# Local heads' scores as single fp32 matmuls on unsplit q and k, and two key tiles instead of four for the sample

## The chip, the cores and the metric

The kernel runs on one core of one Trainium2 chip. The metric is the time of one execution in device microseconds; lower is better. All arithmetic of the reference is in fp32.

## The reference

One encoder layer is applied to two requests, a prompt of 1024 tokens and a sample of 256, each with the same 16 learned meta tokens in front. The model width is 2048, a head has 128 channels. Eight heads (A) attend to all tokens of their request, with two key/value heads; eight heads (B, "local") attend to the meta tokens and to a window of 8 rows by 16 columns around the token, on a grid 64 columns wide. The sample has four rows, so its window is all rows by 16 columns.

```python
def encoder_layer(h, ...):                       # h: (B, N, 2048), N = 16 + tokens
    u = rms_norm(h, norm_w) @ w_in               # 2048 x 6656
    qa, ka, va, za, qb, kb, vb, zb = split(u)
    qa, ka = rope(rms_norm(qa)), rope(rms_norm(ka))          # per head
    ya = global_gqa(qa, ka, va) * silu(za)
    qb, kb = rms_norm(qb), rms_norm(kb)                      # per head
    yb = neighbourhood_attention(qb, kb, vb, rpb) * silu(zb)
    return h + concatenate([ya, yb]) @ w_out

def attend(qb, kidx, bidx):                      # in neighbourhood_attention
    s_win = einsum('bqhd,bqwhd->bhqw', qb, kx[:, kidx]) * scale + rpb_flat[:, bidx]
    s_meta = einsum('bqhd,bkhd->bhqk', qb, km) * scale
    p = softmax(concatenate([s_meta, s_win]))
    return p_meta @ vm + p_win @ vx[:, kidx]
```

## The kernel before

The host reorders tokens into strips of eight columns and puts them in two chunks: chunk 1 has the sample (256 tokens), the first 240 tokens of the prompt and the meta tokens, 512 in all; chunk 2 has the other 784 tokens of the prompt. For each chunk the projection runs over strips of 128 output channels (`strips`, L204 to L206), which are the columns of one head for q, k, v or z. The result of a strip is normalised on the way out of PSUM (`qk_evac`, `v_rows`, `z_evac`).

Most products on TensorE are made of three. An fp32 operand is split into a high half `hi` (a ScalarE copy to the type fp32r, L56) and a low half `lo` (VectorE's difference, L57); the product is `hi hi + hi lo + lo hi`. So there are three matmuls per product in the projection, in the scores and in the output projection (L920 to L922). Some products are done on unsplit fp32 operands in one matmul instruction: P·V of the local heads (L405 for the sample, L465 for the prompt), and the transposes of V (L246, L486).

Attention is interleaved with the projection. The sample's attention runs in chunk 1, head by head after its strips; that of the local heads is `attend_sample`. It cuts the 64 columns of the grid into four windows of 16 query columns (64 queries each) with 32 key columns (128 keys, starting at `32 * w0` for `w0` in `WIN0 = (0, 1, 3, 4)`), which overlap: four key tiles, each with three matmuls of 64 queries (L380 to L382), and V turned to key-major form by one transpose per window (L246). The scores on the meta tokens are three matmuls more (`meta_scores`, L266 to L268).

The prompt's local heads run in `attend_strip`, in 32 blocks: eight heads with four windows each. A block has four key tiles `t`; tiles 0 and 3 meet 128 queries, tiles 1 and 2 meet 192. Each takes three matmuls, L431 to L433, which read q as strided pieces of 64 columns. P·V is one fp32 matmul for each tile, L465. The local heads' q and k of chunk 2 are stored unsplit in DRAM (`q2d`, `k2d`), those of chunk 1 split (`qd`, `kd`); `k_load` and `q_load` fetch both parts for one head, and `split_in_place` (L752, L753) splits the 784 columns of chunk 2. Pools `k`, `q` and `tab` have one buffer each in this half. The last head's four blocks run between the first eight steps of the output projection.

The softmax's largest value and sum go through a reduction over partitions on GpSimd (L278, L295). A TileContext with a scheduler decides the order of the instructions on each engine and in the DMA queue, which all DMAs share (SP); PSUM has two buffers for scores (`sp`), one for P·V (`op`) and one for transposes (`tp`).

Of the kernel before, what the change touches and what calls it, by code (L numbers as in the profile page):

```python
# [38 lines left out]
QB = 256  # L39
WIN0 = (0, 1, 3, 4)  # L40
WTYPE = (0, 1, 1, 2)
FILL = 1
# [7 lines left out]
class Kern:  # L50
# [320 lines left out]

    def attend_sample(self, q, zs, k, meta, vals, vmeta, tab, ydst):

        nc = self.nc
        qh, ql = q[:, 0, :], q[:, 1, :]
        ps = self.sp.tile([P, 2, QB], F32, tag="sp", name="sp")
        for w, w0 in enumerate(WIN0):
            o, c = 32 * w0, slice(64 * w, 64 * w + 64)
            kh, kl = k[:, 0, o:o + P], k[:, 1, o:o + P]
            nc.tensor.matmul(ps[:, 0, c], kh, qh[:, c], start=True, stop=False)  # L380
# [4 lines left out]
        s = s[:, 0, :]  # L385
        for i in range(2):

            v = slice(128 * i, 128 * i + 128)
            nc.vector.scalar_tensor_tensor(out=s[:, v].rearrange("p (w c) -> p w c", w=2),
                                           in0=ps[:, 0, v].rearrange("p (w c) -> p w c", w=2),  # L390
                                           scalar=SCALE, in1=tab[:, i:i + 2, 64:128], op0=ALU.mult, op1=ALU.add)
        m1 = self.t.tile([P, QB], F32, tag="t", name="m1")
        nc.vector.tensor_copy(m1[:], s)
        ma = self.all_max(m1, sm)
        nc.vector.tensor_tensor(out=s, in0=s, in1=ma[:], op=ALU.subtract)
        nc.scalar.activation(s, s, AF.Exp)
        pm3 = self.meta_probs(sm, ma, 1.0)
        a1 = self.t.tile([P, QB], F32, tag="t", name="a1")
        nc.vector.tensor_copy(a1[:], s)
        tot = self.all_sum(a1, sm)  # L400
        po = self.op.tile([P, QB], F32, tag="po", name="po")
        nc.tensor.matmul(po[:], vmeta, pm3[:], start=True, stop=False)
        for w in range(4):
            c = slice(64 * w, 64 * w + 64)
            nc.tensor.matmul(po[:, c], vals[:, w, :], s[:, c], start=False, stop=w == 3)  # L405
        self.put_y(po, tot, zs, ydst)

    def attend_strip(self, q, zs, k, meta, vals, vmeta, tab, w, ydst):

        nc = self.nc
        qv = q[:].rearrange("p i (g r) -> p i g r", g=4)[:, :, :, 64 * w:64 * w + 64]
        groups = {0: (0, 2), 3: (2, 4), 1: (0, 3), 2: (1, 4)}
        pa = self.sp.tile([P, 2, QB], F32, tag="sp", name="sp")
# [9 lines left out]
        for t in (0, 3, 1, 2):  # L425
            a, e = groups[t]
            dst = part(pa, pb, t)
            o = NMETA + 256 * t + 32 * WIN0[w]
            kh, kl = (k[:, i, o:o + P] for i in range(2))
            qh, ql = (qv[:, i, a:e, :] for i in range(2))  # L430
            nc.tensor.matmul(dst, kh, qh, start=True, stop=False)  # L431
            nc.tensor.matmul(dst, kh, ql, start=False, stop=False)
            nc.tensor.matmul(dst, kl, qh, start=False, stop=True)  # L433
            if t == 3:
# [33 lines left out]

    def bias_table(self, h):

        tab = self.tab.tile([P, 3, 384], F32, tag="bt", name="bt")
        with self.tc.issue_after(self.lastw):
            self.nc.sync.dma_start(tab[:], self.io["bt"][h])
        return tab
# [85 lines left out]
    def chunk1(self):  # L560
# [10 lines left out]
        PM = NS + C1P  # L571

        def k_strip(s, g, wc, rope):
            kt_ = self.k.tile([P, 2, T1], F32R, tag="k1", name="kc1")
# [8 lines left out]
        def v_strip(s, g):  # L583
            loc = g > 1
            vs = self.v.tile([P, 4, P], F32 if loc else F32R, tag="v0", name="vs")
# [61 lines left out]
        for h in range(8):  # L647
            kj, qj = k_strip(KB + h, 2 + h, kwb, False), q_strip(QB_ + h, 8 + h, qwb, False)
            k, = pr(kj)
# [5 lines left out]
            else:  # L655
                (v, vm), z = pr(vj, zj)
            run(8 + h, q, z, k, v, vm, self.bias_table(h))


    def chunk2(self):  # L660
# [88 lines left out]

        def split_in_place(t):  # L750

            nc.scalar.copy(t[:, 0], t[:, 1].bitcast(F32))  # L752
            nc.vector.tensor_tensor(out=t[:, 1], in0=t[:, 1].bitcast(F32), in1=t[:, 0].bitcast(F32), op=ALU.subtract)  # L753

        def k_load(g):
            k, km = k_first(g)
            nc.sync.dma_start(k[:, 1, K0:].bitcast(F32), self.k2d[g][:])
            split_in_place(k[:, :, K0:])
            return k, km

        def q_load(h):
            q = self.q.tile([P, 2, NP], F32R, tag="q", name="q")
            nc.sync.dma_start(q[:, :, :C1P].bitcast(F32), self.qd[h][:])
            nc.sync.dma_start(q[:, 1, C1P:].bitcast(F32), self.q2d[h][:])
            split_in_place(q[:, :, C1P:])
            return q

# [8 lines left out]
        def run_block(h, b, q, z, k, v, tab):  # L776
            k, km = k
            v, vm = v
            if tab is not None:
                c = slice(64 * b, 64 * b + 64)  # L780
                self.attend_strip(q, strips_of(z[:])[:, :, c], k, km, v[b], vm[:], tab, b,
                                  strips_of(self.yd[h][:, :NP])[:, :, c])
# [9 lines left out]
        def local_blocks():  # L792
            for h in range(NH):
                k, v = k_load(2 + h), v_windows(h)
                tab, q, z = self.bias_table(h), q_load(8 + h), z_load(8 + h)
                for b in range(4):
# [226 lines left out]
    def build(self):  # L1023
# [3 lines left out]
        with tc.tile_pool(name="dr", bufs=1, space=DRAM) as dp, tc.tile_pool(name="const", bufs=1) as cp, \  # L1027
                tc.tile_pool(name="raw", bufs=3) as self.raw, tc.tile_pool(name="w", bufs=4) as self.w:
            self.kd = [dp.tile([P, 2, NMETA + C1P], F32, name=f"kd{g}") for g in range(10)]
            self.vn = [dp.tile([NP, P], F32, name=f"vn{g}") for g in range(10)]  # L1030
            self.vmd = [dp.tile([M3, P], F32, name=f"vmd{g}") for g in range(10)]
            self.qd = [dp.tile([P, 2, C1P], F32, name=f"qd{h}") for h in range(16)]
            self.zd = [dp.tile([P, NP], F32, name=f"zd{h}") for h in range(16)]
# [11 lines left out]
            with ExitStack() as ps, ExitStack() as es_y:  # L1045
# [22 lines left out]
                pool(es_proj, "ev", 8, side="right", **kw)  # L1068
                for name, bufs in (("k", 1), ("v", 1), ("tab", 1), ("q", 1), ("z", 1), *work, ("y", 1)):
                    pool(es_attn, name, bufs, **kw)  # L1070
# [54 lines left out]


def _lay(x):
    return np.ascontiguousarray(x.reshape(x.shape[0], KT, P).transpose(2, 1, 0))
# [33 lines left out]
```

## Time and profile before

| what | value |
|---|---|
| median of 3 runs | 2222.22 us (2219.42 to 2223.22) |
| profiled execution | 2220.95 us |
| its span | 2219.1 us |
| VectorE busy | 74% of the span |
| ScalarE busy | 51% |
| GpSimd busy | 24% |
| TensorE's granted clock, mean | 0.998 |
| bytes moved by DMA | 391.21 MB |

The span runs from the first to the last instruction; what lies around it is 1.85 us. In the profile PE is TensorE's matmul, PEld its loading of weights (which runs beside PE), DVE is VectorE, ACT ScalarE, POOL GpSimd and SP the engine that issues the DMAs. A group of instructions is named by its line, its engine, what it writes and reads (`out<-in`) and its shape. Durations of matmuls overlap, since the engine is pipelined. In the chain of work that ended last, each piece lasts from the end of the piece before it to its own.

### The profile page before, as it was taken

The numbers are of one execution on the slowest core, as the hardware profiler recorded it, in microseconds if no ns is written. First come the engines' busy times: TensorE is split into PE (matmuls) and PEld (weight loads), VectorE is DVE, ScalarE is ACT, GpSimd is POOL, SyncE is SP. The second block draws the span as 40 slices with busy tenths as digits, with TensorE's granted clock in tenths as the row PEclk, the third lists the DMA queues.
The fourth block names the chain that finished last, engine by engine and source line by source line (L and its number), as shares of the span: only waits on it lengthen the run. The fifth ranks groups of instructions, "written<-read, shape, count | busy, mean of one in ns | idle before, by whom it ended". The sixth has DMA issues, their size and how long they took to land.

```text
span 2219.1 us, 36801 instructions
## 1 busy us (share of the span) xinstructions
PE 2194.2 (99%) x13064; PEld 1982.6 (89%) x13064; DVE 1646.5 (74%) x2911; ACT 1130.9 (51%) x2304; POOL 523.9 (24%) x249
## 2 busy tenths in 40 slices
PE   8999999999999999999999999999999999999999
PEld 7888788888888999999999999999888889999999
DVE  8687876788864899976899988867768766536743
ACT  7555454455554767655666656544434454232220
POOL 1232421222211332321332223423423412000000
PEclk9999999999999999999999999999999999999999
DMA  8767899998465333334333336544433464745663
GB/s 300 220 190 228 273 306 320 320 310 280 148 205 153 103 110 114 99 112 141 102 111 108 102 118 187 177 145 140 132 121 108 138 229 135 235 145 162 206 209 110
DMA packets 269784, 391.21 MB, mean 176 GB/s; under 512 B 46976, under 2 KB 124448, under 8 KB 269600
## 3 DMA queue, kind: packets, MB, share of 16 engines
q1 hardware_dynamic: 269600, 388.86, 54.9%
q8 instruction: 102, 1.67, 0.3%
q14 instruction: 82, 0.67, 0.1%
HBM read 286.19 MB, written 102.42 MB: 175 GB/s over the span
## 4 chain that ended last, share of the span: by engine, by line
PE 91%; DVE 3%; DMA 3%; issue 1%; ACT 1%; POOL 0%; SPq 0%; DVEq 0%; POOLq 0%; ACTq 0%
PE pp L204 20%; PE pp L206 20%; PE pp L205 20%; PE pq L921 6%; PE pq L922 6%; PE pq L920 6%; PE po L465 2%; PE sp L328 1%; PE sp L327 1%; PE sp L326 1%; PE po L368 1%; PE po L366 1%; PE po L367 1%; DVE wl L57 1%; DMA wr<-in_w_in 1%
## 5 line engine op out<-in xcount | busy, mean ns | idle before, releaser
L204 PE MATMUL pp<-x,wh 128*128 128x512 f32 (+1 forms) x2496 | 890.3, 358 | 9.1 <-ACT wh L56 6.3
L206 PE MATMUL pp<-x,wl 128*128 128x512 f32 (+1 forms) x2496 | 890.5, 357 | 0.0
L205 PE MATMUL pp<-x,wh 128*128 128x512 f32 (+1 forms) x2496 | 887.7, 356 | 0.0
L204 PEld LDWEIGHTS pp<-x,wh 128*128 128x128 f32 x2496 | 468.8, 188 | 69.9 <-ACT wh L56 7.7
L205 PEld LDWEIGHTS pp<-x,wh 128*128 128x128 f32 x2496 | 470.4, 188 | 60.4 <-DVE x L101 0.2
L206 PEld LDWEIGHTS pp<-x,wl 128*128 128x128 f32 x2496 | 469.2, 188 | 61.7 <-DVE wl L57 1.2
L57 DVE TENSOR_TENSOR wl<-wr,wh 128x512 fp32r<-128x512 f32 (+1 forms) x402 | 292.1, 739 | 131.1 <-ACT wh L56 108.5
L56 ACT CAST wh<-wr 128x512 fp32r<-128x512 f32 (+1 forms) x402 | 240.1, 611 | 222.5 <-PE pp L205 155.2
L214 POOL PARTITION_ALL_REDUCE m<-ms x78 | 231.6, 2969 | 405.8 <-ACT ms L212 368.4
L295 POOL PARTITION_ALL_REDUCE tot<-a x80 | 181.8, 2273 | 472.6 <-DVE a L293 456.6
L921 PE MATMUL pq<-ym,wh 128*128 128x320 f32 x896 | 277.2, 309 | 2.1 <-DVE ym L57 2.1
L920 PE MATMUL pq<-ym,wh 128*128 128x320 f32 x896 | 277.2, 310 | 0.4 <-ACT ym L56 0.4
L922 PE MATMUL pq<-ym,wl 128*128 128x320 f32 x896 | 276.9, 309 | 0.7 <-DVE wl L57 0.7
L278 POOL PARTITION_ALL_REDUCE ma<-m x80 | 101.5, 1268 | 424.8 <-DVE m L276 423.5
L921 PEld LDWEIGHTS pq<-ym,wh 128*128 128x128 f32 x896 | 168.6, 188 | 2.9 <-DVE ym L57 2.9
L920 PEld LDWEIGHTS pq<-ym,wh 128*128 128x128 f32 x896 | 168.5, 188 | 1.2 <-ACT ym L56 1.0
L922 PEld LDWEIGHTS pq<-ym,wl 128*128 128x128 f32 x896 | 168.5, 188 | 0.9 <-DVE wl L57 0.9
L330 ACT COPY S<-sp 128x512 f32<-128x512 f32 x136 | 78.7, 582 | 57.1 <-PE sp L328 52.0
L189 ACT CAST wh<-wr 128x512 fp32r<-128x512 f32 x132 | 81.6, 618 | 50.9 <-PE pp L205 47.6
L57 DVE TENSOR_TENSOR pl<-S,ph 128x512 fp32r<-128x512 f32 x136 | 97.7, 731 | 9.7 <-ACT ph L56 9.3
L346 DVE TENSOR_TENSOR S<-S,ma 128x512 f32<-128x512 f32 x136 | 98.4, 779 | 8.8 <-POOL ma L278 8.8
L56 ACT CAST ph<-S 128x512 fp32r<-128x512 f32 x136 | 83.4, 615 | 33.2 <-PE po L367 32.2
(207 smaller groups left out, 3320.7 us busy)
## 6 DMA issues: line engine op xcount, KB each, us to landing
wr<-in_w_in SPq DMA_DIRECT2D x414, 256.0 KB, 3.8
wld<-wl SPq DMA_DIRECT2D x132, 256.0 KB, 4.7
wl<-wld SPq DMA_DIRECT2D x132, 256.0 KB, 3.2
wq<-in_w_out SPq DMA_DIRECT2D x64, 256.0 KB, 5.3
td<-wq SPq DMA_DIRECT2D x64, 256.0 KB, 4.2
wr<-td SPq DMA_DIRECT2D x64, 256.0 KB, 3.3
yr<-yd SPq DMA_DIRECT2D x48, 320.0 KB, 3.8
wr<-in_w_out SPq DMA_DIRECT2D x48, 256.0 KB, 4.0
```

Source lines behind the costliest of these rows:

```text
L56: self.hi = nc.scalar.copy(hi, full).ins
L57: return nc.vector.tensor_tensor(out=lo, in0=full, in1=hi.bitcast(F32), op=ALU.subtract).ins
L204: nc.tensor.matmul(p[:, :n], wh[:, k, :], xh[:, :n], start=first, stop=False)
L205: nc.tensor.matmul(p[:, :n], wh[:, k, :], xl[:, :n], start=False, stop=False)
L206: nc.tensor.matmul(p[:, :n], wl[:, k, :], xh[:, :n], start=False, stop=last)
L214: nc.gpsimd.partition_all_reduce(m2[:], ms[:], P, RED.add)
L278: nc.gpsimd.partition_all_reduce(ma[:], m1[:], P, RED.max)
L295: nc.gpsimd.partition_all_reduce(tot[:], a1[:], P, RED.add)
L346: nc.vector.tensor_tensor(out=s, in0=s, in1=mb, op=ALU.subtract)
L920: nc.tensor.matmul(ps[:, b, :B], wh, yh[:, o], start=k == 0, stop=False)
L921: nc.tensor.matmul(ps[:, b, :B], wh, yl[:, o], start=False, stop=False)
L922: nc.tensor.matmul(ps[:, b, :B], wl, yh[:, o], start=False, stop=k == 7)
```

## The change

The scores of the local heads are no longer made of three matmuls on split halves: q and k stay unsplit and each key tile takes one matmul on fp32 operands. For the prompt that is four matmuls per block in place of twelve. Its scores on the meta tokens stay three split ones, so q is still split, all 1024 columns at once, into a tile beside the unsplit one (a new pool `qf` with one buffer); of k only the 16 meta columns are split. In chunk 1 k and q of the local heads are not split at all: `kb_strip` and `qb_strip` take the place of `k_strip` and `q_strip` there, and the parts kept for chunk 2 are stored once in place of twice.

For the sample, the grid is cut into two key tiles of 32 columns that don't overlap; each meets 192 queries (three quarters), so the two score matmuls have 192 columns each, and so have the two of P·V. The two tiles share the middle 128 queries, whose largest values and sums are joined by `gather`. V takes two transposes in place of four. The meta scores are one fp32 matmul, into a PSUM buffer of their own. The bias is read from a table `bs` made on the host, 384 columns wide.

```diff
-    def qk_evac(self, ps, o, n, wc, rope, segs):
+    def qk_evac(self, ps, o, n, wc, rope, segs, full=None):
...
-            nc.vector.scalar_tensor_tensor(out=r[:], in0=ps[:, :n], scalar=wc, in1=r[:], op0=ALU.mult, op1=ALU.mult)
+            d = r[:] if full is None else full
+            nc.vector.scalar_tensor_tensor(out=d, in0=ps[:, :n], scalar=wc, in1=r[:], op0=ALU.mult, op1=ALU.mult)
...
-        for w, w0 in enumerate(WIN0):
-            o, c = 32 * w0, slice(64 * w, 64 * w + 64)
-            kh, kl = k[:, 0, o:o + P], k[:, 1, o:o + P]
-            nc.tensor.matmul(ps[:, 0, c], kh, qh[:, c], start=True, stop=False)
-            nc.tensor.matmul(ps[:, 0, c], kh, ql[:, c], start=False, stop=False)
-            nc.tensor.matmul(ps[:, 0, c], kl, qh[:, c], start=False, stop=True)
-        sm = self.meta_scores(ps[:M3, 1, :], meta, qh, ql, SCALE)
+        for i in range(2):
+            nc.tensor.matmul(ps[:, HALF * i:HALF * i + HALF], k[:, P * i:P * i + P], q[:, 64 * i:64 * i + HALF], start=True, stop=True)
+        pm = self.sp.tile([P, 2, QB], F32, tag="sp", name="sm_ps")
+        nc.tensor.matmul(pm[:M3, 0, :], km, q, start=True, stop=True)
...
+        def gather(name, op):
+
+            m = self.t.tile([P, QB], F32, tag="t", name=name)
+            nc.vector.tensor_copy(ap(m[:], 0, [[192, 2], [1, 64]]), ap(s, 0, [[320, 2], [1, 64]]))
+            nc.vector.tensor_tensor(out=m[:, 64:192], in0=s[:, 64:192], in1=s[:, 192:320], op=op)
+            return m
...
-        for w in range(4):
-            c = slice(64 * w, 64 * w + 64)
-            nc.tensor.matmul(po[:, c], vals[:, w, :], s[:, c], start=False, stop=w == 3)
+        for i in range(2):
+            nc.tensor.matmul(po[:, 64 * i:64 * i + HALF], vals[:, i, :], s[:, HALF * i:HALF * i + HALF], start=False, stop=i == 1)
...
-            kh, kl = (k[:, i, o:o + P] for i in range(2))
-            qh, ql = (qv[:, i, a:e, :] for i in range(2))
-            nc.tensor.matmul(dst, kh, qh, start=True, stop=False)
-            nc.tensor.matmul(dst, kh, ql, start=False, stop=False)
-            nc.tensor.matmul(dst, kl, qh, start=False, stop=True)
+            nc.tensor.matmul(dst, k[:, o:o + P], qfv[:, a:e, :], start=True, stop=True)
...
+        def kb_strip(s, g, wc):
+            kf = self.k.tile([P, T1], F32, tag="k1", name="kcf")
+
+            def evac(ps):
+                self.qk_evac(ps[0], 0, T1, wc, None, [], kf[:])
+                nc.sync.dma_start(self.kfd[g][:, :NMETA], kf[:, PM:])
+                nc.sync.dma_start(self.kfd[g][:, NMETA:], kf[:, NS:PM])
...
+        def qb_strip(s, h, wc):
...
+                self.qk_evac(ps[0], o, n, wc, None, [], q[:, :n])
+                nc.sync.dma_start(self.qfd[h][:], q[:, NS:n])
...
-                    nc.scalar.copy(vs[:], self.v_turn(vt, [32 * w0 for w0 in WIN0]))
+                    nc.scalar.copy(vs[:], self.v_turn(vt, [0, P]))
...
         def k_load(g):
-            k, km = k_first(g)
-            nc.sync.dma_start(k[:, 1, K0:].bitcast(F32), self.k2d[g][:])
-            split_in_place(k[:, :, K0:])
-            return k, km
+            k = self.k.tile([P, NMETA + NP], F32, tag="k1", name="kfull")
+            nc.sync.dma_start(k[:, :K0], self.kfd[g][:])
+            nc.sync.dma_start(k[:, K0:], self.k2d[g][:])
+            km = self.k.tile([P, 2, 3, NMETA], F32R, tag="km", name="km")
...
         def q_load(h):
+            qf = self.qf.tile([P, NP], F32, tag="qf", name="qfull")
+            nc.sync.dma_start(qf[:, :C1P], self.qfd[h][:])
+            nc.sync.dma_start(qf[:, C1P:], self.q2d[h][:])
             q = self.q.tile([P, 2, NP], F32R, tag="q", name="q")
-            nc.sync.dma_start(q[:, :, :C1P].bitcast(F32), self.qd[h][:])
-            nc.sync.dma_start(q[:, 1, C1P:].bitcast(F32), self.q2d[h][:])
-            split_in_place(q[:, :, C1P:])
-            return q
+            self.split(q[:, 0, :], q[:, 1, :], qf[:])
+            return q, qf
```

More of the change, by code (lines that the diff above doesn't have):

```diff
@@ L40 @@
 WIN0 = (0, 1, 3, 4)
+HALF = 192
 WTYPE = (0, 1, 1, 2)
@@ L370, in attend, with attend_sample @@
         self.put_y(po, tot, zs, ydst)
-    def attend_sample(self, q, zs, k, meta, vals, vmeta, tab, ydst):
+    def attend_sample(self, q, zs, k, km, vals, vmeta, tab, ydst):
         nc = self.nc
-        qh, ql = q[:, 0, :], q[:, 1, :]
         ps = self.sp.tile([P, 2, QB], F32, tag="sp", name="sp")
-        for w, w0 in enumerate(WIN0):
-            o, c = 32 * w0, slice(64 * w, 64 * w + 64)
-            kh, kl = k[:, 0, o:o + P], k[:, 1, o:o + P]
-            nc.tensor.matmul(ps[:, 0, c], kh, qh[:, c], start=True, stop=False)
-            nc.tensor.matmul(ps[:, 0, c], kh, ql[:, c], start=False, stop=False)
-            nc.tensor.matmul(ps[:, 0, c], kl, qh[:, c], start=False, stop=True)
-        sm = self.meta_scores(ps[:M3, 1, :], meta, qh, ql, SCALE)
-        s = self.s.tile([P, 2, QB], F32, tag="S", name="S")
[L385 to L396, printed above, removed]
@@ new lines, in attend_sample, with ap @@
+        s = s[:].rearrange("p a b -> p (a b)")
+        w = 2 * HALF
+        nc.vector.scalar_tensor_tensor(out=s[:, :w], in0=ps[:, :w], scalar=SCALE, in1=tab, op0=ALU.mult, op1=ALU.add)
+        def ap(t, off, dims):
+            return bass.AP(t.tensor, t.offset + off, [list(t.ap[0])] + dims)
+        def gather(name, op):
[3 more added lines that the diff above has]
+            return m
@@ L397, in attend_sample @@
+        ma = self.all_max(gather("m1", ALU.max), sm)
+        v = ap(s, 0, [[HALF, 2], [1, HALF]])
+        nc.vector.tensor_tensor(out=v, in0=v, in1=ap(ma[:], 0, [[64, 2], [1, HALF]]), op=ALU.subtract)
+        nc.scalar.activation(s[:, :w], s[:, :w], AF.Exp)
         pm3 = self.meta_probs(sm, ma, 1.0)
-        a1 = self.t.tile([P, QB], F32, tag="t", name="a1")
-        nc.vector.tensor_copy(a1[:], s)
-        tot = self.all_sum(a1, sm)
+        tot = self.all_sum(gather("a1", ALU.add), sm)
         po = self.op.tile([P, QB], F32, tag="po", name="po")
@@ L402, in attend_sample, with attend_strip @@
         nc.tensor.matmul(po[:], vmeta, pm3[:], start=True, stop=False)
-        for w in range(4):
-            c = slice(64 * w, 64 * w + 64)
-            nc.tensor.matmul(po[:, c], vals[:, w, :], s[:, c], start=False, stop=w == 3)
+        for i in range(2):
+            nc.tensor.matmul(po[:, 64 * i:64 * i + HALF], vals[:, i, :], s[:, HALF * i:HALF * i + HALF], start=False, stop=i == 1)
         self.put_y(po, tot, zs, ydst)
-    def attend_strip(self, q, zs, k, meta, vals, vmeta, tab, w, ydst):
+    def attend_strip(self, q, qf, zs, k, meta, vals, vmeta, tab, w, ydst):
@@ L466, in attend_strip, with bias_table @@
         self.put_y(po, tot, zs, ydst)
-    def bias_table(self, h):
-        tab = self.tab.tile([P, 3, 384], F32, tag="bt", name="bt")
+    def bias_table(self, h, name, shape):
+        tab = self.tab.tile([P, *shape], F32, tag="bt", name=name)
         with self.tc.issue_after(self.lastw):
-            self.nc.sync.dma_start(tab[:], self.io["bt"][h])
+            self.nc.sync.dma_start(tab[:], self.io[name][h])
         return tab
@@ L571, in chunk1, with evac @@
         PM = NS + C1P
+        def kb_strip(s, g, wc):
[4 more added lines that the diff above has]
+                nc.sync.dma_start(self.kfd[g][:, NMETA:], kf[:, NS:PM])
+                km = self.k.tile([P, 3, NMETA], F32, tag="km", name="kmf")
+                nc.scalar.copy(km[:], kf[:, PM:].unsqueeze(1).to_broadcast([P, 3, NMETA]))
+                return kf, km[:].rearrange("p c m -> p (c m)")
+            return s, [B0], evac
+        def qb_strip(s, h, wc):
+            q = self.s.tile([P, 2, QB], F32, tag="S", name="qs")
+            q = q[:].rearrange("p a b -> p (a b)")
+            def evac(ps):
+                o, n = BQ
+                self.qk_evac(ps[0], o, n, wc, None, [], q[:, :n])
+                nc.sync.dma_start(self.qfd[h][:], q[:, NS:n])
+                return q[:, :NS]
+            return s, [BQ], evac
         def k_strip(s, g, wc, rope):
@@ L748, in z_late @@
             return s, BL, evac
-        def split_in_place(t):
-            nc.scalar.copy(t[:, 0], t[:, 1].bitcast(F32))
-            nc.vector.tensor_tensor(out=t[:, 1], in0=t[:, 1].bitcast(F32), in1=t[:, 0].bitcast(F32), op=ALU.subtract)
         def k_load(g):
-            k, km = k_first(g)
-            nc.sync.dma_start(k[:, 1, K0:].bitcast(F32), self.k2d[g][:])
-            split_in_place(k[:, :, K0:])
-            return k, km
+            k = self.k.tile([P, NMETA + NP], F32, tag="k1", name="kfull")
+            nc.sync.dma_start(k[:, :K0], self.kfd[g][:])
+            nc.sync.dma_start(k[:, K0:], self.k2d[g][:])
+            km = self.k.tile([P, 2, 3, NMETA], F32R, tag="km", name="km")
+            full = k[:, :NMETA].unsqueeze(1).to_broadcast([P, 3, NMETA])
+            nc.scalar.copy(km[:, 0], full)
+            nc.vector.tensor_tensor(out=km[:, 1], in0=full, in1=km[:, 0].bitcast(F32), op=ALU.subtract)
+            km = km[:].rearrange("p i c m -> p i (c m)")
+            return k, (km[:, 0], km[:, 1])
         def q_load(h):
+            qf = self.qf.tile([P, NP], F32, tag="qf", name="qfull")
+            nc.sync.dma_start(qf[:, :C1P], self.qfd[h][:])
+            nc.sync.dma_start(qf[:, C1P:], self.q2d[h][:])
             q = self.q.tile([P, 2, NP], F32R, tag="q", name="q")
-            nc.sync.dma_start(q[:, :, :C1P].bitcast(F32), self.qd[h][:])
-            nc.sync.dma_start(q[:, 1, C1P:].bitcast(F32), self.q2d[h][:])
-            split_in_place(q[:, :, C1P:])
-            return q
+            self.split(q[:, 0, :], q[:, 1, :], qf[:])
+            return q, qf
         def z_load(h):
@@ L1028, in build @@
                 tc.tile_pool(name="raw", bufs=3) as self.raw, tc.tile_pool(name="w", bufs=4) as self.w:
-            self.kd = [dp.tile([P, 2, NMETA + C1P], F32, name=f"kd{g}") for g in range(10)]
+            self.kd = [dp.tile([P, 2, NMETA + C1P], F32, name=f"kd{g}") for g in range(2)]
+            self.kfd = [dp.tile([P, NMETA + C1P], F32, name=f"kfd{g}") for g in range(10)]
             self.vn = [dp.tile([NP, P], F32, name=f"vn{g}") for g in range(10)]
             self.vmd = [dp.tile([M3, P], F32, name=f"vmd{g}") for g in range(10)]
-            self.qd = [dp.tile([P, 2, C1P], F32, name=f"qd{h}") for h in range(16)]
+            self.qd = [dp.tile([P, 2, C1P], F32, name=f"qd{h}") for h in range(8)]
+            self.qfd = [dp.tile([P, C1P], F32, name=f"qfd{h}") for h in range(16)]
             self.zd = [dp.tile([P, NP], F32, name=f"zd{h}") for h in range(16)]
@@ L1068, in build @@
                 pool(es_proj, "ev", 8, side="right", **kw)
-                for name, bufs in (("k", 1), ("v", 1), ("tab", 1), ("q", 1), ("z", 1), *work, ("y", 1)):
+                for name, bufs in (("k", 1), ("v", 1), ("tab", 1), ("q", 1), ("z", 1), *work, ("y", 1), ("qf", 1)):
                     pool(es_attn, name, bufs, **kw)
@@ L1124, in _bias, with _bias_sample @@
     return np.where(ok, rpb[:, dr, dc], np.float32(NEG)).reshape(NH, P, 3, 384)
+def _bias_sample(rpb):
+    i, a, b = np.meshgrid(np.arange(4), np.arange(4), np.arange(8), indexing="ij")
+    i, kr, b = (x.reshape(-1)[:, None, None, None, None, None] for x in (i, a, b))
+    t, w, h, qr, c = np.meshgrid(*(np.arange(n) for n in (2, 3, 2, 4, 8)), indexing="ij")
+    kc, qc = 32 * t + 8 * i + b, 16 * (t + w) + 8 * h + c
+    c0 = np.clip(qc - 8, 0, 48)
+    ok = (kc >= c0) & (kc < c0 + 16)
+    dr, dc = kr - qr + 7, np.clip(kc - qc + 15, 0, 30)
+    return np.where(ok, rpb[:, dr, dc], np.float32(NEG)).reshape(NH, P, 2 * HALF)
 def _lay(x):
```

17 lines of the change are left out of this document (11 added, 6 removed).

## The prediction

> **What bounds the kernel now.** I read the page first: the busy shares, the slices, and the chain that ended last.
>
> ```profile
> span 2219.1 us, 36801 instructions
> ...
> PE 2194.2 (99%) x13064; PEld 1982.6 (89%) x13064; DVE 1646.5 (74%) x2911; ACT 1130.9 (51%) x2304; POOL 523.9 (24%) x249
> ...
> PE   8999999999999999999999999999999999999999
> ...
> PEclk9999999999999999999999999999999999999999
> ...
> PE 91%; DVE 3%; DMA 3%; issue 1%; ACT 1%; POOL 0%; SPq 0%; DVEq 0%; POOLq 0%; ACTq 0%
> ```
>
> PE is busy in every slice, at a full clock, and carries 91% of the chain. There is one limit from end to end: a microsecond of matmul time taken out is a microsecond of the whole, unless PE then has to wait. So the second view is the list of who waited for whom, cut to PE (columns: us in total, times, longest). Three of its rows bear on the change:
>
> ```profile
> PE pp L204 <- ACT x L153: 2.7, 3, 1.6
> ...
> PE sp L432 <- DVE q L753: 1.5, 1, 1.5
> ...
> PE tp L246 <- DVE vt L239: 1.1, 2, 0.9
> ```
>
> All are small, so the gain has to come mainly from matmul time.
>
> **What one matmul costs.** The third view is the groups by form. It tells how many records a matmul leaves:
>
> ```profile
> L465 PE MATMUL po<-S,vw 128*128 128x192 f32 x128 | 26.1, 326 | 0.0
> L465 PE MATMUL po<-S,vw 128*128 128x128 f32 x128 | 19.4, 274 | 0.0
> L433 PE MATMUL sp<-q,kf 128*128 128x192 f32 x64 | 18.0, 281 | 0.0
> ...
> L405 PE MATMUL po<-S,vs 128*128 128x64 f32 x64 | 8.0, 268 | 0.0
> ```
>
> The code issues L465 64 times in each width (32 blocks, two of each) and the trace has 128 records: a matmul on unsplit fp32 leaves two. L433, on split halves (fp32r), is issued 64 times and leaves 64. The means of 270 to 330 ns overlap each other, so they are not the cost. The cost is the step from one end to the next, which the chain in order of time gives (start, us, what). First a block of the prompt's local heads:
>
> ```profile
> 1373.84 1.10 PE po L465 x8
> 1374.94 0.06 PE sp L431
> ...
> 1375.55 0.12 PE sp L266
> ...
> 1378.04 0.09 PE sp L431
> ...
> 1378.68 0.25 PE pp L204
> 1378.93 0.23 PE pp L205
> ```
>
> Six split score matmuls of 128 queries take 1374.94 to 1375.55, 0.61 us; six of 192 take 1378.04 to 1378.68, 0.64, and the matmul behind them is 0.02 longer than its neighbour. That is 1.27 us a block for twelve, 0.11 each whatever the width. Beside it stand four unsplit matmuls, two of 128 and two of 192 columns, eight records in 1.10 us. Next the sample's P·V and its scores:
>
> ```profile
> 307.51 0.84 PE po L405 x8
> 308.35 0.28 PE pp L205
> 308.63 0.22 PE pp L206
> ```
>
> ```profile
> 292.58 0.03 PE sp L380
> ...
> 293.84 0.13 PE sp L266
> ...
> 294.20 0.23 PE pp L204
> ...
> 295.60 0.44 PE tp L246 x4
> ```
>
> Eight unsplit records of 64 columns take 0.84 us and make the next matmul 0.06 longer: 0.90, or 0.11 a record. So 0.11 is a floor, for split and unsplit alike. If the 128-column records of L465 sit on it too, the 192-column ones take (1.10 - 4 x 0.11) / 4 = 0.165, which is no longer the floor but grows with the columns. An unsplit matmul then costs 0.22 us at 128 columns and 0.33 at 192, where three split ones cost 0.33 at either width. At 256 columns no row shows it: in proportion 2 x 0.22 = 0.44, at the least the 0.36 of the three split ones (293.84 to 294.20).
>
> **The change, part by part.** All on PE, in us, before less after:
> - Prompt's local scores, 32 blocks: twelve split matmuls at 1.27 become four unsplit, the same widths as L465, at 1.10. 32 x 0.17 = **-5.4**. They read q through the same four strided pieces as now, which costs the split ones nothing over the floor; I charge none. Each block gets two new fp32 groups between split ones. Their edges cost between +0.06 (behind L405) and -0.05 (the first split matmul behind a wide one costs 0.06 instead of 0.11, above), so 64 edges are worth +3.8 to -3.2; I take 0, since the 1.10 already holds L465's own.
> - Sample's scores, 8 heads: twelve at 1.26 (292.58 to 293.84) become two of 192 columns, 0.66. 8 x 0.60 = **-4.8**.
> - Sample's P·V: four matmuls of 64, 0.90, become two of 192, 0.66: **-1.9**.
> - Sample's V transposes: four become two, 0.44 to 0.22: **-1.8**.
> - Sample's meta scores: three split at 0.36 become one unsplit, 0.44: **+0.6** (0 at the low end).
>
> Together -13.3 us of PE time.
>
> At one place a rule speaks against this. The Trainium skill, page "FP8 and Floating Point Precision", section "TensorE Precision Notes", says that true fp32 takes four passes through the array (high and low halves, all four products). Four passes in place of three would lose by a third. The trace agrees on four in this sense only: two records whose 192-column length is what four streams of columns would take; but the three split matmuls sit on the floor and do not get cheaper below 256 columns. What the rule makes of the sum at one floor per pass is the slower rival below.
>
> **Waits that go.** The row that shows PE held by L432 is at the last local head, at the start of the output projection:
>
> ```profile
> 1819.31 0.98 DVE q L753
> 1820.34 0.33 PE sp L432
> ...
> 1821.11 0.21 PE sp L266
> ```
>
> ```profile
> 1818.00:1830.00 12.00, 10.54 (x68) 10.12 (x67) 10.62 (x20) 7.97 (x14) 1.50 (x1) 0.86 1.01 342
> ```
>
> Scores wait there for DVE's half of q's split, and then the clock is low: L266 takes 0.21 instead of 0.12, and the windows view has 0.86 granted over those 12 us (the column after POOL's), worth up to 12 x 0.14 = 1.7. After the change the scores need only q and k as loaded; the meta scores still need the split, which grows from 784 columns to 1024, 0.98 to 1.28. In the built order of the changed kernel PE has four scores (1.10), one meta matmul and four of the projection (0.7) before the first that needs DVE's half: 1.8 against 1.5 + 0.3. The wait is just covered. At the first sample head, the built order puts the evacuation of v (L239) ahead of the attention output that held DVE up, so L246's 0.9 should go. In all up to 1.5 + 1.7 + 0.9 = 4.1; I take **-2.5**, because cover that is only just enough often isn't.
>
> **What costs nothing, and what hides it.** On ACT and DVE the splits of k go, and those of q on the sample's side too. These rows are for one k of the prompt:
>
> ```profile
> L752 ACT CAST kf<-kf x8: 847/850/854, 1348.9 to 1812.5; 128x784 fp32r<-128x784 f32 x8
> L753 DVE TENSOR_TENSOR kf<-kf x8: 955/975/979, 1349.8 to 1814.1; 128x784 fp32r<-128x784 f32 x8
> ```
>
> Both engines have room (51% and 74%), so 0.85 and 0.98 saved eight times are worth nothing by themselves; they shorten the way from k's landing to the first score, which is hidden by projection matmuls at seven heads of eight. The sample's softmax on DVE works on 384 columns with two more small operations; its result is wanted 32 to 66 projection matmuls later. On SP there are eight DMAs fewer, and k, q and the sample's bias table move fewer bytes. One thing moves there: q of the first local head has a buffer of its own now, so its second half is loaded right behind the store of the same data, and SP's queue, with weight loads behind it, waits for that store to land.
>
> ```profile
> q<-q2d SPq DMA_DIRECT2D x8, 392.0 KB, 5.9
> ...
> q2d<-rs_r SPq DMA_DIRECT2D x8, 136.0 KB, 2.3
> ```
>
> That is 2.3 us once. The weights loaded ahead (four buffers, each for 24 matmuls, some 4 us) cover it; without them it would be +2.3.
>
> **The sum.** -13.3 - 2.5 = -15.8. The profiled execution took 2220.95 us, so 2205.2. The median of the runs shown is 1.3 above that execution; with it the forecast is **2206 us**. Bounds of the terms: +3.8 at the edges and no wait gone gives 2220.95 - 9.5 = 2211; -3.2 and every wait gone gives 2200. Its own range is 2200 to 2212. A measurement of this kernel tells about 0.2%, 4.4 us, from no change.
>
> **Rivals.**
> - *Slower: four floors for an unsplit matmul.* If each new one cost 4 x 0.11 = 0.44 whatever its width, a strip block would take 1.76 instead of 1.27, +15.7; the sample's scores 0.88 for 1.26, -3.0; P·V nothing, transposes -1.8, meta +0.6: +11.5, 2232 us. It decides from a mean of 1.27 / 4 = 0.32 per strip matmul on. For it: the four passes that the Trainium skill names, in the section cited above. Against it: L465 has the same widths at a mean of 0.275. 5%.
> - *Head boundaries.* k and q have one buffer each, so a head's loads start when the last score before it is done, and q takes 5.9 to land. If PE caught up with them at all seven boundaries by 2 us, 14 of the 15.8 are given back: 2219, no change. Against it: in the built order 54 to 113 matmuls stand between (9 us and more) at six of them; only the first has as few as 42 (7.4 us; 52 before the change). 5%.
> - *Half lost.* The wait at L432 stays, the first boundary costs 2 and SP's queue 2.3: 2220.95 - 13.3 + 4.3 = 2212; to 2216 with the edges. 12%.
> - *More.* All three waits quoted at the start go, since ACT and DVE have less to do where the second half begins: -13.3 - 4.1 - 2.7 = -20.1, 2201 us, to 2198 with the better edges. 8%.
>
> The forecast has 70%. The range for 8 in 10 is 2198 to 2216: it leaves out the slower case and the boundaries, 10%, and a tail of the others. Faster by over 0.2% (below 2217.8) are forecast, half lost and more: 0.90; the boundaries are no change: 0.05; slower: 0.05.
>
> **What would show it.** Right: 128 score matmuls in the prompt's local blocks with 256 records, steps of 0.11 at 128 columns and 0.165 at 192; 32 records for the sample's scores at 0.165; PE's busy time down by 13 us, the share still 99%; no PE row with q at the last head. Wrong: steps of 0.22 per record; new rows "PE sp" waiting for DMA of k or q at head boundaries; or a lower granted clock outside the stretch named.

## The result and the profile after

The changed kernel takes 2209.28 us (median of six executions, 2206.77 to 2215.19) where the kernel before, beside it on the same chip, takes 2222.72 (six, 2219.42 to 2226.0). The ratio is 0.9945, interval 0.9928 to 0.9962: 12.2 us less by the ratio, between 8.4 and 16.0; the medians differ by 13.4. Two repetitions beside the experiments gave 0.9952 (0.9934 to 0.9969) and 0.9953 (0.9941 to 0.9966). The profiled execution took 2206.77 us with a span of 2204.7, against 2220.95 and 2219.1: 14.2 us less, 14.4 of it in the span.

The page of the changed kernel: span, engines, PE's slices, and the shares of the chain that ended last.

```profile
span 2204.7 us, 36270 instructions
...
PE 2180.8 (99%) x12816; PEld 1964.3 (89%) x12816; DVE 1634.2 (74%) x2895; ACT 1115.5 (51%) x2272; POOL 525.2 (24%) x249
...
PE   8999999999999999999999999999999999999999
...
PE 89%; DVE 5%; DMA 3%; issue 1%; ACT 1%; POOL 0%; SPq 0%; DVEq 0%; POOLq 0%; ACTq 0%
```

PE's busy time fell by 13.4 us (2194.2 to 2180.8), its share stayed 99%, and DVE and ACT are 12 and 15 us less busy. The groups by form have the records that were to be seen, all of them matmuls of the local heads:

```profile
L434 PE MATMUL sp<-qfull,kfull 128*128 128x192 f32 x128 | 26.1, 325 | 0.0
L434 PE MATMUL sp<-qfull,kfull 128*128 128x128 f32 x128 | 19.7, 274 | 0.0
L380 PE MATMUL sp<-qs,kcf 128*128 128x192 f32 x32 | 7.5, 326 | 0.0
L409 PE MATMUL po<-S,vs 128*128 128x192 f32 x32 | 6.5, 326 | 0.0
L382 PE MATMUL sm_ps<-qs,kmf 128*48 128x256 f32 x16 | 5.1, 398 | 0.0
```

The chain in order of time gives their steps (start, us, what). First a block of the prompt's local heads, then the sample's scores with the meta scores behind them:

```profile
1380.29 0.44 PE sp L434 x4
...
1381.20 0.33 PE sp L434 x2
1381.53 0.11 PE sp L268
1381.64 0.33 PE sp L434 x2
```

```profile
292.61 0.65 PE sp L380 x4
293.26 0.56 PE sm_ps L382 x2
293.82 0.43 PE pp L205
294.26 0.24 PE pp L206
```

```profile
291.50 0.22 PE tp L248 x2
...
307.99 0.65 PE po L409 x4
308.64 0.23 PE pp L205
```

The block's four unsplit matmuls take 0.44 + 0.33 + 0.33 = 1.10 us, as L465 did. The sample's two take 0.65, and the last fence has a head's transposes, 0.22, and its P·V, again 0.65, with no more time at the matmul behind. The single meta matmul, though, takes 0.56 where three split ones took 0.36, and the projection matmul behind it takes 0.43 where its neighbour takes 0.24.

PE's rows in the list of who waited for whom that bear on the change (columns: us in total, times, longest):

```profile
PE po L463 <- DVE Pm L290: 1.4, 1, 1.4
...
PE tp L248 <- DVE vm L58: 0.7, 1, 0.7
...
PE tp L248 <- DVE vt L241: 0.3, 1, 0.3
```

No row names the prompt's q any more; the 1.5 us before the last local head's scores are gone. In the first row, P·V of a prompt block waits for the meta tokens' probabilities; the kernel before has only 0.3 us of that (at L462). The row for `vm` is new too, so these transposes wait 1.0 us in all, where the kernel before has 1.1. The timeline shows where the first row comes from, DVE's and then GpSimd's part of it (start, us, engine, line, operation):

```profile
1585.18 2.27 DVE L295 TENSOR_TENSOR a<-a,Sm 16x256 f32<-16x256 f32 x1
1587.38 0.68 DVE L58 TENSOR_TENSOR wl<-wr,wh 128x512 fp32r<-128x512 f32 x1
1588.09 1.43 DVE L290 TENSOR_TENSOR Pm<-Sm,Pm 16x256 fp32r<-16x256 f32 x1
```

```profile
1584.93 3.24 POOL L215 PARTITION_ALL_REDUCE m<-ms  x1 [2.13 <-DMA yd<-y]
1588.08 1.87 POOL L297 PARTITION_ALL_REDUCE tot<-a  x1
```

Two VectorE operations run long there, beside reductions on GpSimd: the one that writes `a` takes 2.27 us and the one that writes `Pm` 1.43, where each takes about 0.41 in the median. Together that makes `Pm` 2.9 us late, of which PE waits for 1.4. The windows view, the 30 us that hold the last local head, tells of the clock (columns: stretch, length, PE busy, PEld, DVE, ACT, POOL, granted clock, DMA share, GB/s). The first fence is of the kernel before, the second of the changed one:

```profile
1800.00:1830.00 30.00, 26.98 (x169) 25.28 (x170) 24.46 (x42) 19.45 (x37) 6.88 (x3) 0.94 1.00 341
```

```profile
1800.00:1830.00 30.00, 30.00 (x213) 29.93 (x212) 24.96 (x51) 17.74 (x34) 7.94 (x4) 1.00 0.75 254
```

PE no longer has a gap there, and the clock stays full.

### The profile page after: what moved, and what is told of

Its sections match the earlier page's. It is cut to its first block, busy times and chain, and to the rows that moved or that the text cites. A ratio compares the mean times of both kernels' runs of the same rounds, so it can differ in the third digit from the quotient of the medians.

```text
span 2204.7 us, 36270 instructions
## 1 busy us (share of the span) xinstructions
PE 2180.8 (99%) x12816; PEld 1964.3 (89%) x12816; DVE 1634.2 (74%) x2895; ACT 1115.5 (51%) x2272; POOL 525.2 (24%) x249
## 4 chain that ended last, share of the span: by engine, by line
PE 89%; DVE 5%; DMA 3%; issue 1%; ACT 1%; POOL 0%; SPq 0%; DVEq 0%; POOLq 0%; ACTq 0%
PE pp L205 20%; PE pp L207 20%; PE pp L206 19%; PE pq L947 6%; PE pq L948 6%; PE pq L946 6%; PE po L466 2%; PE sp L330 1%; PE sp L328 1%; PE sp L329 1%; PE po L368 1%; PE po L369 1%; PE po L370 1%; PE sp L434 1%; DMA wr<-in_w_in 1%
## 5 line engine op out<-in xcount | busy, mean ns | idle before, releaser
L205 PE MATMUL pp<-x,wh 128*128 128x512 f32 (+1 forms) x2496 | 895.2, 360 | 8.7 <-ACT wh L57 7.2
L205 PEld LDWEIGHTS pp<-x,wh 128*128 128x128 f32 x2496 | 469.2, 188 | 72.7 <-ACT wh L57 8.5
L58 DVE TENSOR_TENSOR wl<-wr,wh 128x512 fp32r<-128x512 f32 (+1 forms) x402 | 303.8, 768 | 139.2 <-ACT wh L57 86.5
L280 POOL PARTITION_ALL_REDUCE ma<-m x80 | 108.1, 1351 | 420.7 <-DVE m L278 417.1
L64 ACT ACTIVATE rs_l<-m 128x512 f32<-128x512 f32 (+1 forms) x78 | 43.9, 563 | 124.1 <-DVE m L216 119.4
```

Source lines behind the costliest of these rows:

```text
L58: return nc.vector.tensor_tensor(out=lo, in0=full, in1=hi.bitcast(F32), op=ALU.subtract).ins
L205: nc.tensor.matmul(p[:, :n], wh[:, k, :], xh[:, :n], start=first, stop=False)
L280: nc.gpsimd.partition_all_reduce(ma[:], m1[:], P, RED.max)
```

## The experiments

The theory: the gain is matmul time on PE, the floor of 0.11 us a record, and it comes from the prompt's scores and the sample's tiles as they were summed. Rivals: the gain comes from ACT and DVE, relieved of the splits, or from the one wait; or a microsecond of matmul is worth less here than a microsecond of time.

**The changed kernel again, beside the next three.** 2208.6 us (four executions, 2206.02 to 2212.66; before 2220.66), profiled span 2204.1.

**Prompt's scores split again (e2_strips_split).** The prompt's k is split again too, after it is loaded; all else stays as changed.

```diff
-            nc.tensor.matmul(dst, k[:, o:o + P], qfv[:, a:e, :], start=True, stop=True)
+            kh, kl = (k[:, i, o:o + P] for i in range(2))
+            qh, ql = (qv[:, i, a:e, :] for i in range(2))
+            nc.tensor.matmul(dst, kh, qh, start=True, stop=False)
+            nc.tensor.matmul(dst, kh, ql, start=False, stop=False)
+            nc.tensor.matmul(dst, kl, qh, start=False, stop=True)
```

> The changed kernel, but the prompt's local blocks make their scores of three split matmuls again (k is split after loading); the sample keeps all of the change. Matmul time: twelve at 1.27 us a block in place of four at 1.10, +5.4 us, and up to +7.6 if the wait for the split at the last local head comes back: 2214 to 2217. Rival, only the sample's tiling brought the gain: 2209.

Measured: 2211.21 us (four, 2210.21 to 2212.37), ratio to before 0.9962 (0.9947 to 0.9977); span 2209.1, 5.0 above its neighbour's. By medians the part is worth 2.6 us, under the 5.4 expected; the interval overlaps that of the changed kernel beside it (0.9934 to 0.9969), so the medians alone do not exclude the rival's nothing. The matmuls themselves cost what they should: summed over all steps from one matmul's end to the next, the prompt's scores take 40.4 us against 35.0 in the changed kernel. In return the matmuls of the meta tokens' P·V, which include the wait for `Pm`, take 12.7 us against 14.0, 15.3 and 14.5 in three executions of the changed kernel. So 1 to 3 us of the saving come back as that wait: in this kernel no `Pm` of the prompt's half takes more than 0.42 us, and no row of the waits has the meta tokens' P·V (L467 there) held by it, though one has it held 1.0 us by another operation of DVE. The rest of the gap to the median these runs don't settle. The wait for q did not return, but that says nothing about the changed kernel: here only the split reads the unsplit q, so it is loaded earlier, and DVE's half is done at 1794.5 us, 16 us before the last head's first scores.

**Sample with four tiles of 64 (e3_sample_four).** The scores stay unsplit; the tiling is that of before, with its bias table and without `gather`.

```diff
-        for i in range(2):
-            nc.tensor.matmul(ps[:, HALF * i:HALF * i + HALF], k[:, P * i:P * i + P], q[:, 64 * i:64 * i + HALF], start=True, stop=True)
+        for w, w0 in enumerate(WIN0):
+            o, c = 32 * w0, slice(64 * w, 64 * w + 64)
+            nc.tensor.matmul(ps[:, 0, c], k[:, o:o + P], q[:, c], start=True, stop=True)
...
+            nc.tensor.matmul(po[:, c], vals[:, w, :], s[:, c], start=False, stop=w == 3)
```

> The changed kernel, but the sample keeps unsplit q and k with four key tiles of 64 queries, as before. Matmul time: scores eight records at the floor of 0.11, 0.88 in place of 0.65 a head, P.V 0.90 in place of 0.65, two transposes more at 0.11: 0.70 a head, +5.6 us, 2215. Rival, for the sample the single fp32 matmul brings the gain and the tiling nothing: 2209.

Measured: 2211.51 us (seven, 2208.9 to 2214.31), ratio 0.9962 (0.995 to 0.9974), span 2209.2. The tiling alone is worth 2.9 us by medians and 5.1 by spans, where 5.6 was expected; by the intervals, which overlap, the medians alone do not show it. Here is one head of that kernel in its chain, scores and P·V:

```profile
336.92 0.17 PE sp L380 x2
337.08 0.44 PE tp L248 x4
337.53 0.62 PE sp L380 x6
338.14 0.56 PE sm_ps L382 x2
...
351.50 0.84 PE po L405 x8
352.34 0.28 PE pp L205
```

Four tiles: scores 0.79, transposes 0.44, P·V 0.84 and 0.06 behind it. Two tiles: 0.65, 0.22 and 0.65. Over eight heads the steps differ by 1.2 + 1.6 + 1.5 = 4.3 us from the first profile of the changed kernel; against the one beside it the transposes, with their waits, differ by 0.7, and the sum is 3.4. The sample's change of type has no run of its own; by steps its scores take 9.9 us in the kernel before, 6.4 here and 5.2 in the changed kernel.

**Dead splits (e4_dead_split).** ACT and DVE do the removed splits again, into columns that nobody reads.

```diff
+                self.split(kt_[:, 0, :], kt_[:, 0, :], kf)
...
+                self.split(d[:], d[:], q[:, :n])
...
+            self.split(k[:, 0, K0:], k[:, 0, K0:], kf[:, K0:])
```

> The changed kernel with the splits that it saved put back on ScalarE and VectorE as dead work (k and q of the local heads in the first half, k in the second; results go to spare columns that nothing reads). If the gain is matmul time: 2209, within 3. If it came from relief of ScalarE and VectorE: most of the 13 us comes back, 2220.

Its page:

```profile
span 2207.9 us, 36322 instructions
...
PE 2181.6 (99%) x12816; PEld 1963.3 (89%) x12816; DVE 1645.4 (75%) x2919; ACT 1127.5 (51%) x2296; POOL 535.6 (24%) x249
```

Measured: 2208.87 us (four, 2207.79 to 2209.74), 0.3 above the changed kernel beside it, ratio 0.9951 (0.9936 to 0.9966). DVE and ACT are back within 4 us of their busy time before, and the time is not. By medians the relief is worth nothing that these runs can see; the intervals leave room for some 3 us, but not for most of the 12. The profiled span, though, is 3.8 above its neighbour's, 2.3 of that in the steps of the input projection (1458.1 us against 1455.7). So single spans can differ by some 4 us where the medians agree, and the 5.0 and 5.1 of the two kernels above are little more.

**One width of the prompt's scores issued twice (f1_double128, f2_double192).** Each matmul of that width is repeated, which changes no result.

```diff
+            for _ in range(2 if t in (0, 3) else 1):     # f2: t in (1, 2)
-            nc.tensor.matmul(dst, k[:, o:o + P], qfv[:, a:e, :], start=True, stop=True)
+                nc.tensor.matmul(dst, k[:, o:o + P], qfv[:, a:e, :], start=True, stop=True)
```

> The changed kernel with each unsplit score matmul of 128 queries in the prompt's local blocks done twice, to the same place: 64 matmuls, 128 records more. At 0.11 us a record, all of it on the path: +14.1 us, 2223. At four floors of 0.11 a matmul (0.44): +28, 2237. If PE had slack there: less than 14.

> The same with the matmuls of 192 queries: 128 records more. At 0.163 us a record: +20.9 us, 2230. At four floors: +28, 2237; at the floor of two records whatever the width: +14, 2223.

The chain of the first, then of the second:

```profile
1380.56 0.89 PE sp L435 x8
...
1381.57 0.65 PE sp L435 x4
```

```profile
1380.34 0.45 PE sp L435 x4
...
1380.90 1.30 PE sp L435 x8
```

0.89 / 8 = 0.111 us a record at 128 columns and 1.30 / 8 = 0.163 at 192. All steps added, the 128 further records of f1 cost 14.3 us and those of f2 20.8. That settles the price, and the rival of four floors (0.44 a matmul) with it: one matmul is 0.22 and 0.33.

The times rose by less: f1 2219.58 us (ten, 2217.32 to 2222.34; before 2220.0; ratio 0.9998, 0.9989 to 1.0007), f2 2223.44 (ten, 2220.27 to 2226.6; ratio 1.0019, 1.001 to 1.0028). Against the ratio of 0.9952 for the changed kernel that is about 10 and 15 us. The spans, 2216.6 and 2221.6, are 12 and 17 above the mean of the changed kernel's three (2204.7, 2204.1, 2204.6). The list of waits says why they are short of 14.3 and 20.8. Neither kernel has a row where the meta tokens' P·V (L464 there) waits for `Pm`. The changed kernel has one in each of three profiled executions, of 1.4 us above, of 1.5 in the one beside g2_meta128 and, in the one beside e2 to e4, of

```profile
PE po L463 <- DVE Pm L290: 2.9, 1, 2.9
```

The meta tokens' P·V takes 12.3 us in f1 and 11.3 in f2, waits included, against 14.6 in the mean of the changed kernel's three: 2.3 and 3.3 us of the added matmuls only fill time in which PE waited for the softmax. In f2 every `Pm` of that half takes 0.42 us, in f1 the longest 0.71, and the operation on `a` keeps its 0.41 in both: with other times of the matmuls, the two no longer meet the reductions in the same way. With that, 12.0 and 17.5 us of span are accounted for. What is left between spans and medians, some 2 us, is not; the changed kernel's executions lie 2 to 3 us above their profiled one in the median, and that wasn't explained.

**Wider meta keys (f3_meta128, f4_meta64, g2_meta128).** The sample's 48 meta keys (three copies of 16) are padded with more copies to 128 and to 64; the added scores are not read. g2_meta128 is f3_meta128 once more, beside the changed kernel.

```diff
-        nc.tensor.matmul(pm[:M3, 0, :], km, q, start=True, stop=True)
+        nc.tensor.matmul(pm[:128, 0, :], km, q, start=True, stop=True)       # f4: pm[:64, 0, :]
...
-                km = self.k.tile([P, 3, NMETA], F32, tag="km", name="kmf")
+                km = self.k.tile([P, 8, NMETA], F32, tag="km", name="kmf")   # f4: 4
```

> The changed kernel with the sample's unsplit meta score matmul widened from 48 to 128 weight columns (the 16 meta keys eight times over; rows over 48 are not read). In the changed kernel's trace this matmul took 0.35 + 0.215 us and made the next one 0.2 longer. Theory, unsplit weights of fewer than 128 columns cost a switch of 0.33 us going in and out: records of 0.215 and a next matmul of 0.23, -2.6 us, 2206.5. Rival, the extra is the change of PSUM tile or the wait for k's copy: steps as before, 2209.

> The same with 64 weight columns; for the steps in the trace, not the time. If anything under 128 columns costs the switch: 0.35, 0.215 and a next matmul of 0.43, as with 48. If the cost is that of columns that don't fill a quarter of the array: 0.215, 0.215, 0.23.

> The changed kernel with the sample's meta keys widened from 48 to 128 columns (the added keys' scores are not read). If the 0.33 us that each head's meta scores lose with 48 columns (0.13 on the first matmul, 0.20 on the matmul behind) is on the path to the end, 8 of them make it 2.6 us faster than the changed kernel, ratio to it 0.9988. Rival: the wait for the softmax behind takes it back, and the two are alike to 0.5 us.

The chain with 128 columns (g2_meta128), and with 64:

```profile
292.20 0.65 PE sp L380 x4
292.85 0.43 PE sm_ps L382 x2
293.29 0.23 PE pp L205
```

```profile
384.40 0.58 PE sm_ps L382 x2
384.98 0.43 PE pp L205
385.40 0.23 PE pp L206
```

With 48 columns it was 0.56 and 0.43, with 128 it is 0.43 and 0.23: 0.33 us less a head for a wider matmul, 2.6 in eight. With 64 columns nothing is won.

As a version to keep, it can't be told from the changed kernel. f3_meta128 took 2206.53 us (five, 2205.36 to 2211.25), ratio to before 0.9946 (0.9933 to 0.996); g2_meta128 2207.4 (five, 2204.23 to 2211.41), 0.9948 (0.9934 to 0.9962), beside 2208.76 and 0.9953 for the changed kernel. Both medians are lower than the changed kernel's, by a bit over one microsecond by the ratios, and the intervals overlap nearly whole. The spans are not lower: 2204.8 and 2206.6 against 2204.6. In g2_meta128's list of waits a part comes back at the P·V behind:

```profile
PE po L407 <- DVE Pm L290: 1.4, 1, 1.4
```

The changed kernel beside it has 0.3 in that row, and so has f3_meta128, which is the same kernel as g2_meta128; where the rest of the 2.6 us goes is not shown. f4_meta64, one execution, took 2209.18 us.

## Why the prediction was right, and what it missed

2206 was forecast, 2209.28 measured, inside the forecast's own range of 2200 to 2212. For the profiled execution it was 2205.2 against 2206.77. Term by term, "measured" being sums of steps between ends of matmuls, after less before unless something else is said:

| term | forecast, us | measured, us |
|---|---|---|
| prompt's scores, matmuls alone | -5.4 | -5.35 (changed kernel less e2) |
| sample's scores | -4.8 | -4.7 |
| sample's P·V | -1.9 | -1.5, and -0.4 at the matmul behind (0.28 to 0.23, eight times) |
| V transposes | -1.8 | -2.3, with their waits (-1.4 and -0.9 in two other executions) |
| sample's meta scores | +0.6 | +3.2 |
| last head: wait for q, low clock | up to -3.2 | -2.3 (the prompt's scores fell by 7.6 with their waits, 42.7 to 35.0; 5.35 is the price) |
| meta tokens' P·V, with its waits for `Pm` | none | +0.6 (+1.9 and +1.1 in two other executions) |

- **PE as the one limit** held: dead work on ACT and DVE costs 0.3 us by medians, added matmuls cost 10 and 15. It held less exactly than "a microsecond is a microsecond": 1 to 3 us went into a wait at one block of the prompt, where two operations of the softmax met reductions on GpSimd. The prediction asked after cover at head boundaries, and it was there; for the P·V inside a block, which has score matmuls of the next block among its cover, it did not ask.
- **The price of an unsplit matmul**, 0.22 at 128 columns and 0.33 at 192, was right, and doubling each width showed it directly. The Trainium skill, page "FP8 and Floating Point Precision", section "TensorE Precision Notes", has four passes for true fp32. The trace agrees: a record of 192 columns takes 0.163 us, or 0.85 ns a column, about twice the 0.45 ns of a split matmul of 512 columns in the projection (0.23 us), which makes two passes in each of two records. No run showed a floor for each pass: that would be 0.44 us a matmul, and 0.22 was measured at 128 columns.
- **The edges**, taken as 0 between +3.8 and -3.2, are not seen in the prompt's scores: 5.35 of the 5.4 are there.
- **The sample's meta scores are the mis-sized term.** In proportion to the columns 0.44 was right for the matmul; a width of 128 has just that. What was not foreseen is that 48 weight columns cost 0.13 more on the way in and 0.20 on the way out: 8 x 0.33 = 2.6 us, which is the difference from +0.6 to +3.2.
- **The waits.** The one for q went, with its low clock, and by the cover that the prediction counted and doubted. PE does four scores, one meta matmul and four of the projection, and L269, the first to need DVE's half of q, begins 0.76 us after that half is done (timeline, as above):

```profile
1807.64 1.22 DVE L58 TENSOR_TENSOR q<-qfull,q 128x1024 fp32r<-128x1024 f32 x1
1807.82 1.26 PE L434 MATMUL sp<-qfull,kfull 128*128 128x128 f32 x8
...
1809.62 0.28 PE L269 MATMUL sp<-q,km 128*48 128x256 f32 x1
```

The 0.9 us for `vt` at the first sample head are gone from there, as forecast. But the same line waits elsewhere now, for `vt` and for `vm`: 1.0, 1.9 and 2.0 us in three executions, against 1.1 before. This part of the 4.1 us was not gained.
- The SP queue's 2.3 us behind the store of q and the loads at head boundaries left no row at the scores: no matmul of L434 is in the list of waits. The first local head's P·V waits 0.2 to 0.6 us at about 1367 us, in two of three executions for the load of `vm`, where the kernel before does not wait; whether the queue is the reason is not shown.

The table's terms add to -12.8 in this execution. The other 1.7 us of the 14.4 lie in places that the prediction doesn't name: 0.8 in the output projection (400.2 to 399.5 us), 0.3 in the prompt's meta scores and 0.4 in the sample's P·V of the heads A are the largest. That the forecast came within 3 us is in part luck: a cost of 2.6 us that it did not have and the wait for `Pm` were partly made up by these. How far one profiled execution can be read shows in the input projection with the start before it: 1463.7, 1461.2 and 1462.7 us in three executions of the changed kernel.

## What to carry to other kernels

In these traces three matmuls on split halves pay off only where their length is set by the columns. Where each sits on the floor of 0.11 us, a single unsplit fp32 matmul of two records is cheaper (0.22 against 0.33 at 128 columns), at 192 it is equal (0.33), and at 256 it is dearer (0.43 against 0.36). So the prompt's gain comes from its 128-column tiles alone: from e2_strips_split to the changed kernel their steps fall from 19.6 to 14.2 us, those of the 192-column tiles stay at 20.8. Fewer, wider tiles brought the sample 3.4 to 4.3 us of steps, not much less than the change of type brought the prompt. A microsecond taken off a full engine shifts everything behind it, and a part can come back where two other engines now meet: look for the waits that the trace of the changed kernel has and the one before has not.

## What was not expected of the hardware

A small VectorE operation can take three times as long beside a reduction on GpSimd, and the one on `a` above took over five times as long. The `Pm` operation (16 x 256) has 80 instances: 67 of the changed kernel take 0.42 us, 13 take 0.9 to 1.4, and each of those 13 overlaps a `PARTITION_ALL_REDUCE`. Of the 67, 12 overlap one too, so it isn't every overlap. As the profile places them, those 12 begin as the reduction does (up to 0.14 us ahead of it) or in its last 0.7 us; 12 of the long ones begin at least 0.46 us into it with 1.3 us or more to come, and the 13th lies across the end of one and the start of the next. The kernel before has 11 long ones too, none of them in the half with the prompt's attention. The Trainium skill, page "GPSIMD Engine Reference", section "Specifications", says that GpSimd shares its way into SBUF with VectorE, in contention with instructions that have two SBUF inputs; `Pm` is made from two, and the rows agree as far as that goes. The row of `Pm` in the changed kernel, min, median and longest in ns, in the half with the prompt's attention:

```profile
L290 DVE TENSOR_TENSOR Pm<-Sm,Pm x34: 414/415/1434, 1313.1 to 1841.3; 16x256 fp32r<-16x256 f32 x34
```

An unsplit fp32 matmul of two records whose weights have 48 or 64 columns makes itself and its successor longer: steps of 0.56 us for its two records and 0.43 for the next matmul with 48 columns, 0.58 and 0.43 with 64, but 0.43 and 0.23 with 128. Split matmuls of 48 columns show nothing of the kind (L268, 0.11 in the block above), nor do the unsplit transposes, of one record each, with 16 and 112 columns (0.11). It isn't the length of the load, which is the same for both (groups by form of PEld, changed kernel; the last column is the idle time before):

```profile
L434 PEld LDWEIGHTS sp<-qfull,kfull 128*128 128x128 f32 x256 | 37.9, 189 | 0.5
...
L269 PEld LDWEIGHTS sm_ps<-q,km 128*48 128x48 f32 x32 | 3.9, 121 | 0.7
...
L382 PEld LDWEIGHTS sm_ps<-qs,kmf 128*48 128x48 f32 x16 | 1.3, 121 | 1.8 <-issue 1.8
```

A load of 48 columns takes 121 ns for the split keys (L269) and for the unsplit ones (L382). What differs is when it starts. In the timeline, PEld stands idle for 0.23 us before L382's loads, which begin only with the matmul itself, and for 0.40 before the load behind it (in brackets). With 128 columns (second fence, g2_meta128's groups) there is no idle time:

```profile
293.19 0.17 PEld L382 LDWEIGHTS sm_ps<-qs,kmf 128*48 128x48 f32 x2 [0.23 <-issue]
293.75 0.19 PEld L205 LDWEIGHTS pp<-x,wh 128*128 128x128 f32 x1 [0.40 <-issue]
```

```profile
L382 PEld LDWEIGHTS sm_ps<-qs,kmf 128*128 128x128 f32 x16 | 2.8, 190 | 0.0
```

The Trainium skill, page "TensorE: Matmul & The Clock Gate", section "Weight-path perf modes — Fast Weight Load (FWL) and DoubleRow", says that the faster load is on at 128 weights of a type other than fp32. That would part split from unsplit at 128 columns, and there the loads take 188 ns (L205) and 189 ns (L434), with no added step between them. So the longer steps are loads that do not run ahead; why they do not stays open.
